# Spread of 1 / rms by float32r identity products, a later gating of the second plain tile, SSM projection chunks of 262, 394 and 392 columns, and another PSUM bank for the last head's norm

## The chip, the core and the metric

The kernel runs on one core of one Trainium2 chip. The metric is the device time of one execution in microseconds (us). The core's engines run side by side, each through its own list of instructions in order: PE (TensorE, matrix products; its weight loads are listed apart as PEld), DVE (VectorE), ACT (ScalarE), POOL (GpSimd) and SP (SyncE, which issues most DMA transfers). An instruction that needs another engine's result waits for it, and everything behind it on its engine waits too.

## The reference, cut to what matters

One step of a hybrid decoder layer on 16 meta tokens, 1024 prompt tokens and 8 sample tokens, 1048 tokens in all, model width 1024:

```python
h = h + 0.5 * swiglu(rmsnorm(h, n1), w1g, w1u, w1d)
u = rmsnorm(h, nm) @ w_in
q, fz, iv, g, z, xbc, dt_raw = jnp.split(u, SPLITS, axis=-1)
...
o_hg = o_hg * lax.rsqrt(jnp.mean(o_hg * o_hg, axis=-1, keepdims=True) + EPS)
o_hg = o_hg.reshape(bsz, seqlen, HG_WIDTH) * hg_norm.astype(f32) * jax.nn.silu(g.astype(f32))
xbc_act, conv_buf = causal_conv(xbc.astype(f32), s_conv.astype(f32), conv_w.astype(f32), conv_b.astype(f32))
...
yz = yz * lax.rsqrt(jnp.mean(yz * yz, axis=-1, keepdims=True) + EPS)
mix = jnp.concatenate([o_hg, yz], axis=-1).astype(h.dtype) @ w_out
h = h + mix
h = h + 0.5 * swiglu(rmsnorm(h, n2), w2g, w2u, w2d)
```

`swiglu(x, wg, wu, wd)` is `(silu(x @ wg) * (x @ wu)) @ wd` with an inner width of 2816. `xbc` (1024 columns) and `dt_raw` (8 columns) are what this page calls the SSM projection. The outputs are the prompt and sample rows after a final norm and the new states.

## The kernel before

Activations are kept transposed: a tile has 128 features on the partitions and tokens along the columns. The token axis has four **quarters** of `Q` = 262 columns in the first half of the kernel (258 after the meta tokens are dropped). Every large product is done as three float32r products (`mm3`, lines 169, 170 and 171): weights and activations are each split into a high part (a cast to float32r, on ACT) and a low part (the rest, a subtraction on DVE), and high x high, high x low and low x high are added up in PSUM. PE therefore needs, for each operand, one ACT and one DVE operation to be done first.

PSUM has two pools here: `mis` with 4 banks (`K.psm()`), and `acc`, with 4 banks outside the feed-forward blocks (`K.psum()`).

**The first feed-forward block** (`ffn`, with `Input` for its input) is written as a list of numbered steps. A step is 12 products of 262 columns on PE; `before(S, i, ...)` places other work ahead of step i, and on one engine the order of these calls is the order of execution. Steps 0 to 31 are two plain tiles (`Plain`): their products run on the input without its norm, since 1 / rms is one number per token and can be multiplied in afterwards. `Input.rms` (step 24) gets 1 / rms of every token, tokens on the partitions; it then writes ten diagonal matrices (`diag`, L1425, on ACT), and `Input.spread_r(q)` (L1430, steps 28 to 31) multiplies a matrix of ones by a quarter of them on PE, in fp32, so that every partition holds 1 / rms along the tokens. L1431 copies that to SBUF. `Plain.late` then multiplies each tile's two halves by it and forms silu(gate) x up (L704, L709, L713 on DVE, 524 columns each; the sub-steps of tile f start at step 33 + 6 f). From step 32 on, pairs of tiles follow (`pair`, `two_pairs`), whose weights are prepared on DVE and ACT at the same time (L493, L497, L501) and whose sums are read from PSUM by DVE (L598, L605, L607, L609).

**From the first block to the SSM projection.** `after1` gets the norm of the block's output a quarter at a time: squares on ACT (L255), sums on DVE (L256), a product with ones on PE (L263), ln and exp on ACT (L185, L186), a Newton step on DVE (L189 to L191), and then eight tiles of normalised x per quarter (`plain_x`: L327 on DVE, L328 high part on ACT, L330 low part on DVE). Quarters 0 and 1 are done during the last steps, quarters 2 and 3 behind them. `ssm_project` multiplies this x by eight units of 128 weight columns. Each unit goes through the token axis in the three chunks of `CHUNKS`, one PSUM bank for each; for the first three units the chunks are the outer loop (`proj_first`), so that chunk 0 of all three comes before chunk 1. `proj_dt` does the 8 columns of dt in the same chunks, and `ssm_decay` (L1540 and after) the small work on dt.

**The last norms.** `Rms` normalises over partitions: `root` sums with four products of 32 output rows (L209) in one bank and takes mean, ln and exp on ACT (L211, L216, L217, with a table load ahead of ln, L214), `newton` has three DVE operations (L221 to L223), and `part` spreads each quarter with one product (L229). Two of them stand at the end of the mixer: that of the SSM group 1 (`ssm_norm`, spreads copied by ACT, L1806) and that of head 3 of the HGRN2 group (`hgrn_out`, spreads read by DVE, L2083). Around them PE works on the first output projection (`out_proj`).

Inside the feed-forward blocks the written order holds for PE, DVE, ACT and SP; in the mixer's middle it holds for PE alone. Elsewhere, at the SSM projection and at the last norms, a scheduler of the language orders the instructions when the kernel is built, from its own estimates. The order on each engine is fixed before the kernel runs.

## Time and profile before

| what | value |
|---|---|
| median of 3 runs | 1921.43 us (1920.21 to 1922.94) |
| the profiled execution | 1922.67 us |
| its span, first to last instruction | 1920.9 us |
| mean granted clock of PE in it | 0.998 |
| PE records, and their busy time | 16692, 1905.5 us |

A row of the timeline has the start of a group of equal instructions in us from the span's start, its length, engine, line, output and input tiles with shapes, and, in brackets, how long the engine had been idle and what released it. Lengths of products overlap: the pace is the distance between two starts. An fp32 product shows two records, a float32r product one. A row of the waits names who waited for whom, for how long in total, how often, and the longest. A row of the stretches has the length, each engine's busy time and number of instructions, the granted clock of PE as a share of full speed, the DMA share and GB/s.

### The profile page before, as it was taken

The page shows a single profiled execution, that of the slowest core. Times are in us where ns is not written, and L with a number is a line of the kernel's source. Part 1 is how long each engine was busy: PE and PEld are TensorE (multiplying, and loading weights), DVE is VectorE, ACT ScalarE, POOL GpSimd, SP SyncE. Part 2 cuts the span into 40 slices and gives each one's busy share as a digit, 9 for nine tenths or more (in the row PEclk, how much of TensorE's full clock was granted, in tenths as well). Part 3 has the DMA queues.
Part 4 walks back from the last instruction along what each step waited for, and adds up shares of the span by engine and source line. Part 5 has one row for each costly group of instructions (what it writes and reads, how often), then busy time and mean ns, then how long its engine had stood idle before and what let it go on. Part 6 is the DMA issues. An engine that isn't in the chain of part 4 may idle for free.

```text
span 1920.9 us, 41195 instructions
## 1 busy us (share of the span) xinstructions
PE 1905.5 (99%) x16692; PEld 1875.2 (98%) x16692; DVE 1526.5 (79%) x2866; ACT 858.0 (45%) x1635; POOL 30.1 (2%) x88
## 2 busy tenths in 40 slices
PE   9999999999999999999999999999999999999998
PEld 9999999999999999999999999999999999999998
DVE  7888888889788877566585557999888888978974
ACT  6533333334534644466564545743333332453353
POOL 3000000000000000000000000000000000000000
PEclk9999999999999999999999999999999999999999
DMA  7143333335967541221463254133333333596852
GB/s 249 50 128 95 95 107 112 92 98 175 305 215 243 165 152 52 66 89 38 116 186 85 83 173 144 58 114 107 99 93 101 101 112 93 173 269 210 281 175 84
DMA packets 324209, 258.46 MB, mean 135 GB/s; under 512 B 18923, under 2 KB 298731, under 8 KB 324011
## 3 DMA queue, kind: packets, MB, share of 16 engines
q1 hardware_dynamic: 323779, 255.79, 43.1%
q8 instruction: 131, 2.15, 0.5%
q14 instruction: 59, 0.48, 0.1%
q0 software_dynamic: 224, 0.04, 0.0%
q10 hardware_dynamic: 16, 0.00, 0.0%
HBM read 190.79 MB, written 65.05 MB: 133 GB/s over the span
## 4 chain that ended last, share of the span: by engine, by line
PE 94%; DVE 3%; ACT 1%; issue 1%; DMA 0%; SPq 0%; DVEq 0%; ACTq 0%
PE acc L169 24%; PE acc L171 23%; PE acc L170 23%; PE mis L169 5%; PE mis L170 5%; PE mis L171 5%; PE mis L1963 1%; DVE u L382 1%; DVE u L367 1%; PE mis L1665 0%; PE mis L2030 0%; PE mis L1659 0%; DMA s<-in_x_prompt_dram 0%; PE mis L2055 0%; PE mis L1654 0%
## 5 line engine op out<-in xcount | busy, mean ns | idle before, releaser
L169 PE MATMUL acc<-u,ws 128*128 128x258 f32 (+4 forms) x3634 | 1064.0, 293 | 1.1 <-DVE u L1279 0.8
L171 PE MATMUL acc<-u,ws 128*128 128x258 f32 (+4 forms) x3634 | 1055.3, 290 | 0.7 <-DVE ws L501 0.7
L170 PE MATMUL acc<-u,ws 128*128 128x258 f32 (+4 forms) x3634 | 1054.8, 290 | 0.0
L169 PEld LDWEIGHTS acc<-u,ws 128*128 128x128 f32 x3634 | 686.5, 189 | 8.7 <-issue 6.2
L170 PEld LDWEIGHTS acc<-u,ws 128*128 128x128 f32 x3634 | 688.3, 189 | 0.8 <-DVE u L330 0.2
L171 PEld LDWEIGHTS acc<-u,ws 128*128 128x128 f32 x3634 | 686.1, 189 | 1.6 <-DVE ws L501 1.1
L169 PE MATMUL mis<-u,ws 128*128 128x262 f32 (+1 forms) x810 | 230.2, 284 | 0.0
L171 PE MATMUL mis<-u,ws 128*128 128x262 f32 (+1 forms) x810 | 228.7, 282 | 0.0
L170 PE MATMUL mis<-u,ws 128*128 128x262 f32 (+1 forms) x738 | 208.6, 283 | 0.0
L501 DVE TENSOR_TENSOR ws<-r,ws 128x512 fp32r<-128x512 f32 x266 | 181.6, 684 | 4.1 <-ACT ws L497 3.9
L901 ACT ACTIVATE t<-t 128x524 f32<-128x524 f32 (+1 forms) x72 | 46.1, 640 | 300.1 <-DVE t L898 300.1
L497 ACT CAST ws<-r 128x512 fp32r<-128x512 f32 x266 | 156.8, 615 | 42.2 <-PE mis L171 18.1
L169 PEld LDWEIGHTS mis<-u,ws 128*128 128x128 f32 x810 | 152.9, 189 | 0.1
L171 PEld LDWEIGHTS mis<-u,ws 128*128 128x128 f32 x810 | 152.7, 189 | 0.0
L170 PEld LDWEIGHTS mis<-u,ws 128*128 128x128 f32 x738 | 139.9, 190 | 0.1
L493 DVE TENSOR_TENSOR r<-r,r 128x512 f32<-128x512 f32 x150 | 100.8, 684 | 0.3
L1031 DVE TENSOR_TENSOR u<-u,u 128x1048 fp32r<-128x1048 f32 (+3 forms) x84 | 96.1, 1146 | 4.8 <-ACT u L1027 4.3
L1089 ACT CAST ws<-u 128x512 fp32r<-128x512 f32 (+1 forms) x72 | 42.1, 585 | 109.9 <-DVE u L1084 105.2
L164 DVE TENSOR_TENSOR ws<-r,ws 128x512 fp32r<-128x512 f32 x88 | 59.5, 685 | 38.3 <-ACT ws L163 38.0
L1027 ACT CAST u<-u 128x1048 fp32r<-128x1048 f32 (+3 forms) x84 | 82.8, 988 | 1.3 <-DMA u<-hd 1.3
L1118 DVE SCALAR_TENSOR_TENSOR s<-acc,s 128x524 f32<-128x524 f32 (+3 forms) x86 | 53.9, 651 | 35.3 <-PE acc L171 35.0
L898 DVE TENSOR_TENSOR t<-t,u 128x524 f32<-128x524 f32 (+1 forms) x108 | 73.2, 692 | 0.1
(465 smaller groups left out, 2329.1 us busy)
## 6 DMA issues: line engine op xcount, KB each, us to landing
r<-in_w_ffn_down_dram SPq DMA_DIRECT2D x128, 256.0 KB
hd<-s SPq DMA_DIRECT2D x93, 258.0 KB
r<-in_w_ffn_gate_dram SPq DMA_DIRECT2D x88, 256.0 KB
r<-in_w_ffn_up_dram SPq DMA_DIRECT2D x88, 256.0 KB
hd<-s SPq DMA_DIRECT2D x77, 262.0 KB
u<-hd SPq DMA_DIRECT2D x36, 516.0 KB
u<-hd SPq DMA_DIRECT2D x28, 524.0 KB
r<-in_w_in_dram SPq DMA_DIRECT2D x56, 256.0 KB
```

Of the source, the lines that this page charges most:

```text
L164: self.nc.vector.tensor_sub(lo, src, hi.bitcast(F32))
L169: mm(ps, whi, xhi, start=first, stop=False, skip_group_check=more)
L170: mm(ps, whi, xlo, start=False, stop=False, skip_group_check=more)
L171: mm(ps, wlo, xhi, start=False, stop=last, skip_group_check=more)
L493: self.K.nc.vector.tensor_tensor(self.raw[p], self.raw[x], self.raw[y], op)
L497: self.K.nc.scalar.copy(self.w[p][:, : self.n * P], self.raw[p])
L501: self.K.nc.vector.tensor_sub(t[:, 512 : 512 + w], self.raw[p], t[:, :w].bitcast(F32))
L898: nc.vector.tensor_mul(t, t if src is None else src, spread.lanes(n, slice(0, 2)))
L901: nc.scalar.activation(t, t, AF.Silu)
L1027: K.nc.scalar.copy(hi, lo.bitcast(F32))
L1031: K.nc.vector.tensor_sub(lo, lo.bitcast(F32), hi.bitcast(F32))
L1118: nc.vector.scalar_tensor_tensor(t, b, 0.5, t, ALU.mult, ALU.add)
```

## The change

The chunks of the SSM projection (all eight units and dt) become 262, 394 and 392 columns:

```diff
+CHUNKS_X = [(0, 262), (262, 394), (656, 392)]
-def proj(K, wh, wl, evac, chunks=CHUNKS):
+def proj(K, wh, wl, evac, chunks=CHUNKS_X):
 def proj_first(K, units):
-    for c in CHUNKS:
+    for c in CHUNKS_X:
 ...
     def proj_dt(c):
-        c0, w = CHUNKS[c]
+        c0, w = CHUNKS_X[c]
```

`Input.rms` no longer writes diagonal matrices. It splits 1 / rms (128 x 10) into a float32r part and a rest, and `spread_r` multiplies one column of each, broadcast over 128 columns as the stationary operand, by columns of a float32r identity matrix that `constants` makes once: for each quarter three pieces (a quarter touches three of the ten token tiles) of two products, 24 products in all. They stand a step later, at steps 29 to 32:

```diff
+    K.identr = cst.tile([P, P], F32R, name="identr")
+    nc.vector.tensor_copy(K.identr, K.ident)
 ...
         token_rstd(K, *(self.st[:, j] for j in range(3)))
-        self.diag = K.slot("u", T)
-        for i, (t0, n) in enumerate(self.tiles):
-            K.nc.scalar.activation(self.diag[:, t0 : t0 + n], K.ident[:, :n], AF.Identity, scale=self.st[:, 1, i : i + 1])
+        self.parts = K.sml.tile([P, 2, 10], F32R, tag="rp", name="rp", bufs=1)
+        K.nc.vector.tensor_copy(self.parts[:, 0], self.st[:, 1])
+        K.nc.vector.tensor_sub(self.parts[:, 1], self.st[:, 1], self.parts[:, 0].bitcast(F32))
     def spread_r(self, q):
         ps = K.psm()[:, :Q]
-        K.nc.tensor.matmul(ps, K.ones[1], self.diag[:, q * Q : q * Q + Q], start=True, stop=True)
+        for i, (t0, n) in enumerate(self.tiles):
+            c0, c1 = max(t0, q * Q), min(t0 + n, q * Q + Q)
+            for j in range(2):
+                if c0 < c1:
+                    K.nc.tensor.matmul(ps[:, c0 - q * Q : c1 - q * Q], self.parts[:, j, i : i + 1].broadcast_to([P, P]), K.identr[:, c0 - t0 : c1 - t0], start=j == 0, stop=j == 1)
         K.nc.scalar.copy(self.spread.quarter(q), ps)
 ...
-            before(S, 28 + q, (x.spread_r, q))
+            before(S, 29 + q, (x.spread_r, q))
```

The gating of the second plain tile starts two steps later, both tiles' gating is placed behind the other work of the same step, and the hidden tiles' sums move with it:

```diff
-                p.late(S, late_r + 6 * f)
-            hidden.jobs(S, 0, hid, late_r + 2, late_r + 10)
+                later.append(lambda p=p, f=f: p.late(S, late_r + 8 * f))
+            later.append(lambda hid=hid: hidden.jobs(S, 0, hid, late_r + 2, late_r + 12))
 ...
+            for fn in later:
+                fn()
+            later = []
```

The root of head 3's norm takes its bank from `acc` in place of `mis`:

```diff
-    def __init__(self, K, v, scale):
-        self.K, self.v, self.scale = K, v, scale
+    def __init__(self, K, v, scale, bank=None):
+        self.K, self.v, self.scale, self.bank = K, v, scale, bank or K.psm
 ...
-        ps = K.psm()[:, :w]
+        ps = self.bank()[:, :w]
 ...
-    rms = Rms(K, v, 1.0 / P)
+    rms = Rms(K, v, 1.0 / P, K.psum if hd == 3 else None)
```

How this moves instructions is shown at three places. In the changed kernel's rows the same code has other line numbers (L169 to L171 are L170 to L172, L209 is L210, L229 is L230, L263 is L264, L1430 is L1440, L1484 is L1494), and the running numbers of the tiles differ.

First PE at the border of the first two chunks of the SSM projection. `u` are the tiles of normalised x (u_8545 and u_8553 are the first tile's high and low part before, u_8559 and u_8567 in the change), `acc` the banks, one for each unit and chunk. Before:

```order
L170 MATMUL acc_9028<-u_8559,ws_8987 128x350
L263 MATMUL mis_8795<-t_8040,ones_85 128x262
L1484 MATMUL mis_8956<-ident,u_8954 128x24 x8
L171 MATMUL acc_9028<-u_8551,ws_8987 128x350
L169 MATMUL acc_9028<-u_8552,ws_8987 128x350
```

In the change:

```order
L171 MATMUL acc_9068<-u_8574,ws_9013 128x262
L172 MATMUL acc_9068<-u_8566,ws_9013 128x262
L264 MATMUL mis_8809<-t_8054,ones_85 128x262
L1494 MATMUL mis_8970<-ident,u_8968 128x24 x8
L170 MATMUL acc_9094<-u_8559,ws_8984 128x394
L170 MATMUL acc_9120<-u_8559,ws_8996 128x394
L170 MATMUL acc_9146<-u_8559,ws_9008 128x394
L171 MATMUL acc_9094<-u_8567,ws_8984 128x394
```

The product for the norm of quarter 2 (L263) and the eight transposes for the convolution (L1484) stood inside the first chunk, with 22 of its products behind them; now they stand behind the whole first chunk, and the second chunk's first products are next.

Second PE at the spread of the first quarter in the first feed-forward block (`rp` holds the two parts of 1 / rms, `mis` the bank). Before, between steps 27 and 28:

```order
L171 MATMUL mis_871<-u_438,ws_609 128x262
L1430 MATMUL mis_886<-u_814,ones_83 128x262
L169 MATMUL acc_825<-u_526,ws_628 128x262
L170 MATMUL acc_825<-u_544,ws_628 128x262
L171 MATMUL acc_825<-u_526,ws_628 128x262
```

In the change, the spreads of quarters 0 and 1 without the steps around them:

```order
L1440 MATMUL mis_893<-identr,rp 128x128 x4
L1440 MATMUL mis_893<-identr,rp 128x6 x2
L1440 MATMUL mis_917<-identr,rp 128x122 x2
L1440 MATMUL mis_917<-identr,rp 128x128 x2
L1440 MATMUL mis_917<-identr,rp 128x12 x2
```

One fp32 product of 262 columns has become six float32r products, of 6 to 128 columns.

Third PE at the two last norms. `t_14251` is 1 / rms of the SSM group before, `t_14265` in the change; `t_14306` is that of head 3 in the change. Before:

```order
L171 MATMUL acc_14381<-u_13582,ws_14331 128x258
L229 MATMUL mis_14260<-t_14251,ones_83 128x258
L229 MATMUL mis_14263<-t_14251,ones_83 128x258
L229 MATMUL mis_14266<-t_14251,ones_83 128x258
L229 MATMUL mis_14269<-t_14251,ones_83 128x258
L209 MATMUL mis_14287<-u_14280,ones_83 32x258 x4
L169 MATMUL acc_14381<-u_13838,ws_14331 128x258
```

In the change (the second root, `acc_14301`, stands 38 rows further up, right behind the first):

```order
L170 MATMUL acc_14395<-u_13596,ws_14345 128x258
L230 MATMUL mis_14274<-t_14265,ones_83 128x258
L230 MATMUL mis_14277<-t_14265,ones_83 128x258
L230 MATMUL mis_14280<-t_14265,ones_83 128x258
L230 MATMUL mis_14283<-t_14265,ones_83 128x258
L230 MATMUL mis_14315<-t_14306,ones_83 128x258
L230 MATMUL mis_14318<-t_14306,ones_83 128x258
L230 MATMUL mis_14321<-t_14306,ones_83 128x258
L230 MATMUL mis_14324<-t_14306,ones_83 128x258
L171 MATMUL acc_14395<-u_13597,ws_14345 128x258
```

The second root has moved ahead of 37 products of the output projection, and head 3's four spreads from 44 products further down to right behind the other four.

More of the change, by code (lines that the diff above doesn't have):

```diff
@@ L1177, in ffn @@
         S.before(32 if plain else 14, lambda: K.banks(2))
-        hidden = Hidden(K)
+        hidden, later = Hidden(K), []
         if plain:
```

## Prediction

> **What bounds the kernel now.** I read the page's busy times and its chain that ended last, then the list of PE's waits, then the timeline around each wait that the change touches.
>
> ```profile
> PE 1905.5 (99%) x16692; PEld 1875.2 (98%) x16692; DVE 1526.5 (79%) x2866; ACT 858.0 (45%) x1635; POOL 30.1 (2%) x88
> ...
> PE 94%; DVE 3%; ACT 1%; issue 1%; DMA 0%; SPq 0%; DVEq 0%; ACTq 0%
> ```
>
> PE is busy for 99% of the span and holds 94% of the chain. So the time changes only by what PE streams more or less of, and by the waits ahead of PE. Those waits are few:
>
> ```profile
> PE acc L169 <- DVE u L1279: 0.8, 1, 0.8
> PE acc L171 <- DVE ws L501: 0.7, 2, 0.4
> ...
> PE mis L209 <- ACT s L1806: 0.4, 1, 0.4
> ```
>
> The change aims at each of them, and at two at L1430 that are quoted below. So each part has the same question: when this wait goes, which one is next?
>
> **Part 1, the SSM projection's chunks.** First the pace of a product: two rows that are 23 products of 262 columns apart, two that are 11 of 350 columns apart, and the entry of the projection.
>
> ```profile
> 682.31 0.28 PE L169 MATMUL acc<-u,ws 128*128 128x262 f32 x1
> ...
> 685.10 0.28 PE L171 MATMUL acc<-u,ws 128*128 128x262 f32 x1
> ...
> 698.67 0.28 PE L171 MATMUL acc<-u,u 128*128 128x262 f32 x1
> 699.74 0.59 PE L169 MATMUL acc<-u,ws 128*128 128x350 f32 x2 [0.78 <-DVE u L1279]
> ...
> 722.68 0.33 PE L169 MATMUL acc<-u,ws 128*128 128x350 f32 x1
> ...
> 724.46 0.32 PE L171 MATMUL acc<-u,ws 128*128 128x350 f32 x1
> ```
>
> A product of 262 columns takes 2.79 / 23 = 0.121 us, one of 350 takes 1.78 / 11 = 0.162 us: in proportion to the columns, as far as these rows tell. All three chunks together have the same columns and the same number of products as before, so streaming gains and loses nothing. What changes is when each operand is needed. The old first chunk (columns 0 to 349) needs quarters 0 and 1 of the normalised x, and PE waits for quarter 1 from 698.79 (698.67 plus one product) to 699.74, and 0.2 more in the next products: 1.2 us. The new first chunk is quarter 0 alone, which is ready, so PE goes on at once. But both the old second chunk (350 to 699) and the new one (262 to 655) reach into quarter 2 (524 to 785). When quarter 2 is ready is told by its chain:
>
> ```profile
> 706.46 0.42 DVE L1118 SCALAR_TENSOR_TENSOR s<-acc,s 128x262 f32<-128x262 f32 x1
> ...
> 706.98 0.42 ACT L255 ACTIVATE t<-s 128x262 f32<-128x262 f32 x1 [0.93 <-DVE lb L1287]
> ...
> 707.42 1.28 ACT L179 ACT_TABLE_LOAD   x1
> 707.43 0.43 DVE L256 TENSOR_TENSOR t<-t,t 128x262 f32<-128x262 f32 x1 [0.27 <-ACT t L255]
> ...
> 708.07 0.60 PE L263 MATMUL mis<-t,ones 128*128 128x262 f32 x2
> 708.61 0.67 PE L1484 MATMUL mis<-ident,u 24*128 24x24 f32 x8
> ...
> 709.48 0.53 ACT L186 ACTIVATE t<-t,lna 128x262 f32<-128x262 f32 x1
> ...
> 711.83 0.90 DVE L327 SCALAR_TENSOR_TENSOR t<-s,col,t 128x262 f32<-128x262 f32 x2
> 712.36 0.82 ACT L328 CAST u<-t 128x262 fp32r<-128x262 f32 x2 [1.75 <-DVE t L327]
> ```
>
> The chain starts on DVE behind quarter 1's tiles and runs DVE, ACT, PE, ACT, DVE, ACT. PE's only link in it, L263 at 708.07, comes right after DVE's L256 ends at 707.86, and the ACT step behind it waits for the table load to 708.70 anyway. DVE's order is the same in the change up to here, so starting PE earlier doesn't start this chain earlier: the first high part of quarter 2 lands at about 712.8 in both kernels. Before, PE reached the second chunk at that very moment, busy throughout. Now: 72 products of 0.121 from 698.8 end at 707.5; the norm's product and the eight transposes (held to 708.07 by L256) end at 709.2; then PE has nothing in its order until 712.8. That is a wait of about 3.6 us, and 0.5 ahead of L263. At 712.8 the old kernel had 72 products of 0.162 behind it, the new one 72 of 0.121: **+2.9 us**, and the 1.2 us at the entry are already in it (they only make the new wait longer). PE's order is fixed, and ahead of quarter 2's first product it holds nothing more. Later DVE delivers one tile of eight in about 0.75 us and the interleaved order uses about 4 products of 394 columns (0.18 each, by proportion) for it, so PE isn't starved again.
>
> The clock is the second half of this part.
>
> ```profile
> 743.82 1.28 PE L1540 MATMUL mis<-sel,u 16*128 16x8 f32 x10
> ...
> 744.00:747.40 3.40, 3.40 (x28) 3.11 (x28) 1.89 (x6) 2.46 (x3) 0.00 (x0) 1.00 0.52 139
> 747.40:750.80 3.40, 3.40 (x12) 3.40 (x13) 3.30 (x13) 0.27 (x1) 0.00 (x0) 0.50 0.60 162
> 750.80:754.20 3.40, 3.40 (x22) 3.40 (x22) 2.92 (x15) 0.45 (x1) 0.00 (x0) 1.00 0.29 85
> ```
>
> After 3.4 us in which most records are 8-column scraps, the granted clock is 0.50 for 3.4 us, and 12 products run where the next stretch has 22: (22 - 12) x 0.162 = 1.6 us lost. In the change PE would stream only some 0.6 us between 707.5 and 712.8, thinner than that stretch, so I expect the clock to halve once: between 0.8 us (half of the stretch falls into the wait) and 2.5 us (a second stretch), I take **+1.6**. If instead only a stretch without any work halves the clock, the wait of 3.6 us would hardly ever cover a whole one of 3.4, and the term is 0; the stretch ahead of 747.4 wasn't without work, so I follow the row and keep the other as a rival. The Trainium skill ("TensorE: Matmul & The Clock Gate", Part 1 and "HAM oscillation — how this bites in real kernels") speaks for that rival: it has the gate look at free-running windows of about 3.4 us and warns of idle gaps above that length, by which the sum would lose its 1.6.
>
> **Part 2, the spread of 1 / rms.** The four fp32 products and what surrounds them:
>
> ```profile
> 59.77 0.28 PE L171 MATMUL mis<-u,ws 128*128 128x262 f32 x1
> 60.45 0.71 PE L1430 MATMUL mis<-u,ones 128*128 128x262 f32 x2 [0.40 <-ACT u L1425]
> ...
> 64.24 0.28 PE L171 MATMUL acc<-u,ws 128*128 128x262 f32 x1
> 65.02 0.71 PE L1430 MATMUL mis<-u,ones 128*128 128x262 f32 x2 [0.49 <-ACT u L1431]
> ...
> 67.59 0.28 PE L170 MATMUL mis<-u,ws 128*128 128x262 f32 x1
> ```
>
> From 59.77 to 67.59 are 7.82 us with 38 main products, which take 38 x 0.121 = 4.6; so 3.2 us go to the spread. The waits are 60.45 - 59.89 = 0.56 and 65.02 - 64.36 = 0.66; the products are the other 2.0. Both waits go: the ten ACT pieces are gone, one step more lies ahead, and DVE gets two operations of 10 columns in their place, a step before they are read. The new price is 24 products with a 128-column stationary operand, 16 of 122 to 128 columns and 8 of 6 or 12. No float32r product under 256 columns is in the trace. Low: 128 columns in proportion to 262, 0.06 each, 24 x 0.06 = 1.4. Nearest row: the ten L1540 records above also have 128 stationary columns and stream only 8; they take 1.28 us with the last one's tail, so about 0.12 each, and 24 x 0.12 = 2.9. High: the fp32 price, two such records for each wide product, 16 x 0.24 + 8 x 0.12 = 4.8. I take 2.9, as the stationary operand has the same width: 2.9 - 3.2 = **-0.3**, from -1.8 to +1.6.
>
> **Part 3, the gating two steps on.** It moves three of DVE's 524-column operations behind the weight's low half that PE waited for.
>
> ```profile
> 78.00:107.70 29.70, 29.26 (x239) 28.93 (x237) 29.53 (x49) 10.67 (x19) 0.00 (x0) 1.00 0.33 105
> ...
> 87.26 0.39 PE L171 MATMUL acc<-u,ws 128*128 128x262 f32 x1 [0.44 <-DVE ws L501]
> ...
> 107.05 0.69 DVE L607 TENSOR_TENSOR t<-acc,t 128x524 f32<-128x524 f32 x1
> ...
> 107.89 0.36 PE L169 MATMUL acc<-u,ws 128*128 128x262 f32 x1
> ```
>
> The wait ahead of 87.26 (0.6 us) goes. But DVE is busy 29.53 of 29.70 us here, and from the start of this stretch to the read of the bank at 107.05 the change has the very same operations, in another order. PE's product at 107.89 waits for that read, so PE arrives earlier and waits longer: **0**. If DVE weren't the limit there, the gain would be the 0.6 plus the two waits behind it, 0.9.
>
> **Part 4, the last norm's bank.**
>
> ```profile
> 1147.72 1.28 ACT L214 ACT_TABLE_LOAD   x1
> 1149.01 0.42 ACT L216 ACTIVATE t<-t 128x258 f32<-128x258 f32 x1
> 1149.46 0.51 ACT L217 ACTIVATE t<-t,lna 128x258 f32<-128x258 f32 x1
> ...
> 1151.29 0.43 DVE L223 SCALAR_TENSOR_TENSOR t<-t,t 128x258 f32<-128x258 f32 x1
> ...
> 1151.87 0.72 PE L229 MATMUL mis<-t,ones 1*128 1x258 f32 x8
> 1153.00 0.64 PE L209 MATMUL mis<-u,ones 128*32 128x258 f32 x8 [0.42 <-ACT s L1806]
> ```
>
> The second root (L209) no longer waits for a bank, so the 0.46 us between the two rows go. But PE's order now has all eight spreads in a row, and the last four need the second norm's Newton steps. On ACT these come after the first norm's exp, which ends at 1149.97 in the row and some 0.2 later behind the second root's copy, and after another table load of 1.28: with ln (0.42) and exp (0.51) they end at 1152.4. Three DVE operations of 0.46 (L223 and the two ahead of it) give 1153.8. PE is through with the first four spreads at 1152.59 in the row, and 0.3 later now (the root of 0.57 ahead of them, two products fewer): a new wait of 0.9. So 0.9 - 0.46 = **+0.4**, from -0.5 (no new wait) to +0.8.
>
> **Sum.** +2.9 + 1.6 - 0.3 + 0 + 0.4 = +4.6 us. Against the profiled execution (1922.67, span 1920.9 and 1.8 around it) that is 1927.3. That execution holds the half-clock stretch at 747.4, which need not fall into every run; the median of the runs shown is 1921.43, so I forecast **1926.0**.
>
> **Rivals.**
> - *The wait comes, the clock stays* (only a stretch without any work halves it): +2.9 - 0.3 + 0.4 = +3.0, 1924.4. For it: the gap is broken by the norm's product at 708.07. Against: the row at 747.4.
> - *Narrow float32r products cost the fp32 price*: 4.8 - 3.2 = +1.6 in place of -0.3, 1927.9. For it: nothing in the trace but fp32 at this width; against: each fp32 product shows two records, a float32r one shows one.
> - *Not slower: quarter 2 isn't late.* If its chain is released by PE and moves up with it, the entry's 1.2 us are kept and no wait and no half clock follow: -1.2 - 0.3 + 0.4 = -1.1, 1920.3. It decides once quarter 2's first cast ends before 709.2. Against: DVE's L1118 at 706.46 sits behind quarter 1's tiles.
> - *The gating's gain stays* (DVE reaches L607 earlier): -0.9, 1925.1.
>
> **How the numbers follow.** Forecast 0.55, clock stays 0.20, narrow price 0.13, not late 0.07, gating 0.05. Measurements of this kernel tell 0.2% (3.8 us) from no change, so slower means above 1925.27: the forecast's upper 70% (0.39), nearly all of the narrow price (0.12) and a little of the rest (0.04) make 0.55; within 0.2% is 0.42; faster needs two rivals at once, 0.03. The range: down to 1922.5 (clock stays, with spread at its low bound), up to 1928.6 (second stretch of half clock, or the narrow price).
>
> **What would show it.** Right: a wait of 3 to 4 us on PE after the eight 24-column transposes, ended by the cast of quarter 2; a stretch at 0.50 clock behind it; no wait at the projection's entry, nor at the spread; a longer wait near 107; about 1 us of wait among the eight spreads near 1153. Wrong: quarter 2's cast earlier by more than 1 us, or PE filling the gap with other products.

## The result, and the profile after

| | before | changed |
|---|---|---|
| median (us) | 1921.82, 6 executions, 1920.21 to 1923.08 | 1930.51, 6 executions, 1927.76 to 1932.03 |
| span of the profiled execution (us) | 1920.9 | 1929.1 |

The ratio is 1.0045, with a 95% interval of 1.0032 to 1.0058: 8.7 us slower, between 6.1 and 11.1. The forecast was 1926.0, 4.6 us slower than the kernel before. The direction is right, and the time lies above the range.

The page of the changed kernel (its busy times, and its chain of work that ended last) reads as before: PE sets the end.

```profile
PE 1908.8 (99%) x16708; PEld 1879.8 (97%) x16708; DVE 1526.7 (79%) x2869; ACT 855.8 (44%) x1625; POOL 32.5 (2%) x88
...
PE 93%; DVE 4%; ACT 2%; DMA 1%; issue 1%; DVEq 0%; SPq 0%; ACTq 0%
```

PE's waits in the changed kernel (who waited for whom, total, times, longest):

```profile
PE acc L170 <- ACT u L329: 3.5, 1, 3.5
PE mis L1640 <- DVE s L1665: 2.1, 2, 2.0
...
PE mis L230 <- DVE t L224: 1.4, 1, 1.4
...
PE acc L170 <- DVE t L608: 0.5, 1, 0.5
```

The first is the border of the chunks, the third the eight spreads of the last norms, the fourth the gating: all three forecast. The second stands in the SSM scan, which the change does not touch. (`ssm_scan` goes through nine blocks of 128 tokens. For each, SP loads `cumd`, a small table of cumulated decays, spread over the partitions: one transfer at L1622, two at L1629. ACT reads the first at L1647.)

To see where the time goes, take the start of the same PE product in both profiles:

| place | before | changed | later by | since the row above |
|---|---|---|---|---|
| a transpose of the input (L1343) | 15.36 | 14.59 | -0.76 | -0.8 |
| first main product after the four spreads | 70.75 | 69.56 | -1.19 | -0.4 |
| product after the late read of the bank | 107.89 | 106.80 | -1.09 | +0.1 |
| a norm's product (L263) | 644.18 | 644.27 | +0.09 | +1.2 |
| norm of quarter 2 (L263) | 708.07 | 708.12 | +0.05 | 0.0 |
| dt's first small product (L1540) | 743.82 | 748.11 | +4.29 | +4.2 |
| a transpose ahead of the scan (L1526) | 808.01 | 810.84 | +2.82 | -1.5 |
| in the SSM scan (L1654) | 849.05 | 855.65 | +6.60 | +3.8 |
| in the last HGRN2 scan (L1975) | 1107.86 | 1115.03 | +7.17 | +0.6 |
| a norm's product in the second block (L263) | 1197.49 | 1204.83 | +7.33 | +0.2 |
| a transpose near the end (L2135) | 1847.97 | 1856.18 | +8.21 | +0.9 |

The border costs 4.2, the scan 3.8. The -1.5 behind the border is the old half-clock stretch at 747, which this execution does not have; seven of the sixteen profiles here (before, changed, e1 to e14) have one between 745 and 753. The 1.2 from 108 to 644 and the 0.9 at the end build up where PE's order is the same in both kernels and nothing waits.

The border, in the changed kernel's timeline of PE and in three stretches around it:

```profile
708.12 0.71 PE L264 MATMUL mis<-t,ones 128*128 128x262 f32 x2 [0.26 <-DVE t L257]
708.76 0.67 PE L1494 MATMUL mis<-ident,u 24*128 24x24 f32 x8
712.98 1.03 PE L170 MATMUL acc<-u,ws 128*128 128x394 f32 x2 [3.55 <-ACT u L329]
```

```profile
709.42:712.83 3.41, 0.01 (x1) 0.00 (x0) 3.15 (x9) 0.98 (x3) 0.00 (x0) 1.00 0.00 0
713.20:716.60 3.40, 3.40 (x12) 3.40 (x13) 3.40 (x10) 1.78 (x5) 0.00 (x0) 0.55 0.00 0
716.60:720.00 3.40, 3.40 (x21) 3.40 (x20) 3.19 (x9) 1.24 (x3) 0.21 (x4) 1.00 0.02 5
```

PE stands still until 712.98, where the forecast had 712.8, and runs 12 products where the next stretch has 21. The half clock begins at 712.83; the 3.41 us ahead of it hold 0.01 us of PE work.

The scan, in the changed kernel's timeline of SP, ACT and PE:

```profile
836.34 0.33 SPq L1622 DMA_DIRECT2D s<-cumd  x1
837.34 1.23 SPq L1629 DMA_DIRECT2D s<-cumd  x2
```

```profile
842.69 2.44 ACT L1647 ACTIVATE s<-s,s 128x128 f32<-128x128 f32 x8 [3.12 <-DMA s<-cumd]
```

```profile
846.02 0.60 PE L1632 MATMUL mis<-ident,u 128*128 128x128 f32 x4
848.58 0.44 PE L1640 MATMUL mis<-ident,u 128*128 128x128 f32 x2 [1.96 <-DVE s L1665]
```

and the same load and its reader in the kernel before:

```profile
833.50 0.33 SPq L1612 DMA_DIRECT2D s<-cumd  x1
```

```profile
837.33 2.46 ACT L1637 ACTIVATE s<-s,s 128x128 f32<-128x128 f32 x8 [0.60 <-DMA s<-cumd]
```

ACT gets the load 6.35 us after its issue, before 3.8. ACT's exp and DVE's L1665 follow it, L1665 frees the bank that PE's next transposes need, and PE stops for 2.0. The transfers between 837 and 846 of the changed kernel (GB/s in 40 slices, and the queue that fetches instructions), then GB/s of the kernel before at the same distance from its issue (834.16 to 843.16):

```profile
GB/s 0 146 364 309 382 55 0 0 73 164 330 314 332 296 237 121 118 118 66 16 18 18 20 23 20 20 7 0 0 0 0 0 0 0 0 0 0 0 0 0
...
q8 instruction: 1, 0.02, 0.7%
```

```profile
GB/s 0 146 146 364 346 455 309 184 205 205 264 212 175 225 173 121 7 0 0 5 9 9 9 0 0 0 0 0 0 0 36 0 0 0 0 0 0 0 0 0
```

In the changed kernel the load stops for about half a microsecond near 838.5 and ends in a thin tail of 16 to 23 GB/s up to 843; before, it runs through. A packet of the instruction queue, 16 KB and 0.97 us long, starts at 838.93, behind the stop and ahead of the tail. Whether it makes the load late isn't told by these rows; e7 tests it.

### The profile page after: what moved, and what is told of

The parts are those of the page before. It is cut to its first block, busy times and chain, and to the rows that moved or that the text cites. A ratio compares the mean times of both kernels' runs of the same rounds, so it can differ in the third digit from the quotient of the medians.

```text
span 1929.1 us, 41213 instructions
## 1 busy us (share of the span) xinstructions
PE 1908.8 (99%) x16708; PEld 1879.8 (97%) x16708; DVE 1526.7 (79%) x2869; ACT 855.8 (44%) x1625; POOL 32.5 (2%) x88
## 4 chain that ended last, share of the span: by engine, by line
PE 93%; DVE 4%; ACT 2%; DMA 1%; issue 1%; DVEq 0%; SPq 0%; ACTq 0%
PE acc L170 24%; PE acc L172 23%; PE acc L171 23%; PE mis L170 5%; PE mis L172 5%; PE mis L171 5%; PE mis L1973 1%; DMA s<-cumd 1%; PE mis L2040 0%; DVE ws L502 0%; PE mis L2065 0%; PE mis L1962 0%; PE mis L1669 0%; DVE t L328 0%; PE mis L2067 0%
## 5 line engine op out<-in xcount | busy, mean ns | idle before, releaser
L170 PE MATMUL acc<-u,ws 128*128 128x258 f32 (+6 forms) x3634 | 1065.8, 293 | 4.4 <-ACT u L329 3.5
L172 PE MATMUL acc<-u,ws 128*128 128x258 f32 (+6 forms) x3634 | 1056.8, 291 | 0.5 <-DVE ws L502 0.3
L171 PE MATMUL acc<-u,ws 128*128 128x258 f32 (+6 forms) x3634 | 1054.8, 290 | 0.0
L170 PEld LDWEIGHTS acc<-u,ws 128*128 128x128 f32 x3634 | 687.3, 189 | 11.6 <-issue 6.4
L171 PEld LDWEIGHTS acc<-u,ws 128*128 128x128 f32 x3634 | 688.3, 189 | 0.6 <-issue 0.3
L172 PEld LDWEIGHTS acc<-u,ws 128*128 128x128 f32 x3634 | 686.2, 189 | 1.1 <-DVE ws L502 0.9
L172 PE MATMUL mis<-u,ws 128*128 128x262 f32 (+1 forms) x810 | 229.8, 284 | 0.0
L170 PE MATMUL mis<-u,ws 128*128 128x262 f32 (+1 forms) x810 | 229.6, 283 | 0.0
L171 PE MATMUL mis<-u,ws 128*128 128x262 f32 (+1 forms) x738 | 208.5, 283 | 0.0
L170 PEld LDWEIGHTS mis<-u,ws 128*128 128x128 f32 x810 | 153.3, 189 | 0.0
L172 PEld LDWEIGHTS mis<-u,ws 128*128 128x128 f32 x810 | 152.7, 188 | 0.0
L171 PEld LDWEIGHTS mis<-u,ws 128*128 128x128 f32 x738 | 139.8, 189 | 0.0
```

Source lines behind the costliest of these rows:

```text
L170: mm(ps, whi, xhi, start=first, stop=False, skip_group_check=more)
L171: mm(ps, whi, xlo, start=False, stop=False, skip_group_check=more)
L172: mm(ps, wlo, xhi, start=False, stop=last, skip_group_check=more)
```

## The experiments

Times are medians. The kernel before ran beside each group, with 1921.3 to 1922.2 us.

| run | us | ratio to before | 95% interval |
|---|---|---|---|
| e1 changed kernel again | 1932.01 | 1.0053 | 1.0040 to 1.0065 |
| e2 chunks alone | 1928.17 | 1.0031 | 1.0020 to 1.0043 |
| e3 changed, old chunks | 1928.82 | 1.0036 | 1.0022 to 1.0050 |
| e4 changed, four chunks | 1927.57 | 1.0030 | 1.0019 to 1.0042 |
| e5 changed, rp of 128 bytes | 1928.29 | 1.0038 | 1.0026 to 1.0051 |
| e6 a tile of 80 bytes alone | 1923.02 | 1.0009 | 1.0000 to 1.0018 |
| e7 16 more PE records alone | 1925.26 | 1.0020 | 1.0011 to 1.0029 |
| e8 changed, old spread | 1927.65 | 1.0034 | 1.0021 to 1.0047 |
| e9 four chunks and spread | 1923.38 | 1.0010 | 1.0001 to 1.0019 |
| e10 bank alone | 1923.28 | 1.0008 | 0.9999 to 1.0017 |
| e11 gating alone | 1922.20 | 1.0002 | 0.9993 to 1.0012 |
| e12 spread alone, rp of 128 bytes | 1924.17 | 1.0014 | 1.0005 to 1.0023 |
| e13 two units in four chunks | 1923.33 | 1.0006 | 0.9997 to 1.0015 |
| e14 the same and the spread | 1922.34 | 1.0000 | 0.9991 to 1.0009 |

### The changed kernel again (e1), no edit

> The changed kernel as it is, looked at a second time. The first profile of it shows two new stops of PE: 3.46 us at 709.2 (the border of the first two chunks, with a half-clock stretch of 3.4 us behind it) and 2.13 us at 846.4 (in the SSM scan, behind a load of cumd that took some 6.3 us from its issue where the others take 3.7 to 4.1; with a second half-clock stretch behind it). Theory 'border': only the first belongs to the change and the late load is chance: this profile has the wait at 709 and none over 0.5 us near 846, and a span of about 1925. Rival 'scan': the late load comes with the change: the wait of about 2 us near 846 is there again, and the span is about 1929. Timed: 8 to 9 us over the kernel before in both, if the medians of six runs hold.

The scan's wait is there, but of 0.2 us, and the span is 1928.1 nevertheless: a half-clock stretch that lasted 3.4 us behind the border in the first profile lasts 6.8 here, and another stands at 753. The load near 839 takes 4.6 us from issue to landing, where the first profile's took 6.3. So the late load is neither pure chance nor always as late. Both theories miss a part.

### The chunks alone (e2), and all but the chunks (e3)

```diff
 e2: the kernel before, with
+CHUNKS_X = [(0, 262), (262, 394), (656, 392)]
 (as in the change)
 e3: the changed kernel, with
-CHUNKS_X = [(0, 262), (262, 394), (656, 392)]
+CHUNKS_X = CHUNKS
```

> The kernel before with the chunks of 262, 394 and 392 alone. Theory 'border': the wait of some 3.5 us, 0.4 ahead of the norm's product and the half clock behind it cost 4.5 against the old entry; with a half-clock stretch of the old kernel at 747 gone in some runs: 3 to 5 us over the kernel before. Rival 'scan': another 3.7 from the wait near 846: 7 to 9 us. Rival 'elsewhere': if most of the 8.7 us comes from the other three parts, under 3 us.

> The changed kernel with the old chunks of 350, 350 and 348 (spread, gating and bank stay changed). In the first two profiles, set side by side, the spread gained 0.4, the gating gave 0.1 back beyond its gain, the bank cost 0.1 to 0.2: theory 'border' and rival 'scan' both give -0.5 to +0.5 us against the kernel before. Rival 'elsewhere': 4 us or more over it, with a wait that the first profile of the changed kernel doesn't show as new.

The chunks cost 6.2 us, a little above the 3 to 5 of "border". The profile says why in part: two stretches of half clock behind the wait. (It is of the fastest of the six executions, 1926.54; what the median has beyond that no profile shows.)

```profile
708.50:711.90 3.40, 0.59 (x8) 0.49 (x8) 2.56 (x8) 1.22 (x4) 0.00 (x0) 1.00 0.14 56
711.90:718.70 6.80, 6.07 (x18) 6.07 (x19) 6.59 (x18) 3.47 (x9) 0.12 (x4) 0.50 0.00 0
718.70:722.10 3.40, 3.40 (x20) 3.40 (x20) 1.01 (x3) 0.71 (x3) 0.10 (x3) 1.00 0.06 3
```

PE worked for 0.59 us of the stretch ahead of the half clock. It is 0.6 to 0.7 in e1 and e8, which have two stretches as well, and nothing in e5, which has one like the changed kernel. So in these five profiles two follow where the wait covers only a part of the 3.4 us ahead, and one where it covers them whole.

E3 is the surprise: without the chunks the kernel is still 6.8 us slower, which "border" and "scan" both put near 0. Its profile has none of the border's waits, but two in the scan (0.81 and 1.22, at 845 and 864) and a half-clock stretch at 898. (E10 and e11 have one at 892 without these waits, so it need not come from them.) So the scan's waits don't come with the chunks.

### Pace and addresses (e5, e6)

The new tile `rp` (80 bytes a partition, laid out as 96) and the identity (512) move the tiles behind them in SBUF: the activations `u`, PE's moving operands, start 608 bytes later, the weights `ws`, which lie ahead of `rp`, 512. In e5 `u` starts 640 bytes later and `ws` the same 512; in e6 `u` starts 96 bytes later and `ws` stays.

```diff
 e5: the changed kernel, with
-self.parts = K.sml.tile([P, 2, 10], F32R, tag="rp", name="rp", bufs=1)
+self.parts = K.sml.tile([P, 2, 16], F32R, tag="rp", name="rp", bufs=1)[:, :, :10]
 e6: the kernel before, with (in Input.rms)
+pad = K.sml.tile([P, 2, 10], F32, tag="rp", name="rp", bufs=1)
+K.nc.gpsimd.memset(pad, 0.0)
```

> The changed kernel, its new tile rp laid out with 128 bytes a partition in place of 80, so that the activations' tiles behind it start 640 bytes later than in the kernel before (a multiple of 64) in place of 608 (not one). Nothing else differs. In the feed-forward blocks, where the order of PE is the same in all kernels, the pace of a product was 0.12166 us (120 to 400 us of the span) and 0.12169 (400 to 640) before and with the chunks alone, and 0.12198 and 0.12190 in the three profiles that have the new spread. Theory 'address': the pace is set by where the moving operand starts; it is 0.12166 and 0.12169 here again, and the time is about 2 us below the changed kernel (1929 to 1930 where that has 1930.5 to 1932). Rival 'spread itself': the pace comes from the new operations or the identity's 512 bytes; 0.12198 and 0.12190 again, and no gain.

> The kernel before with a tile of 80 bytes a partition at the place where rp would be, set to zero by POOL and never read: the activations' tiles start 96 bytes later, and no other instruction changes. Theory 'address': pace 0.1219 to 0.1220 in the first feed-forward block, and 2 us over the kernel before. Rival 'spread itself': pace 0.12166 and 0.12169, and the time of the kernel before.

Three stretches, in which PE is never idle, in the kernel before, the changed kernel, e5 and e6; the first (x...) is the number of PE's products:

```profile
120.00:400.00 280.00, 280.00 (x2304) 280.00 (x2303) 242.29 (x440) 90.22 (x168) 0.00 (x0) 1.00 0.33 100
400.00:640.00 240.00, 240.00 (x1974) 240.00 (x1974) 204.89 (x323) 105.29 (x175) 0.00 (x0) 1.00 0.68 211
1300.00:1850.00 550.00, 550.00 (x4587) 550.00 (x4586) 472.21 (x802) 203.03 (x355) 0.20 (x1) 1.00 0.49 150
```

```profile
120.00:400.00 280.00, 280.00 (x2298) 280.00 (x2297) 241.50 (x439) 90.25 (x168) 0.00 (x0) 1.00 0.33 99
400.00:640.00 240.00, 240.00 (x1972) 240.00 (x1971) 204.39 (x323) 105.52 (x175) 0.00 (x0) 1.00 0.68 211
1300.00:1850.00 550.00, 550.00 (x4581) 550.00 (x4580) 476.41 (x809) 202.56 (x352) 0.20 (x1) 1.00 0.50 152
```

```profile
120.00:400.00 280.00, 280.00 (x2307) 280.00 (x2306) 242.62 (x441) 90.22 (x168) 0.00 (x0) 1.00 0.33 99
400.00:640.00 240.00, 240.00 (x1974) 240.00 (x1973) 204.74 (x323) 106.60 (x177) 0.00 (x0) 1.00 0.69 213
1300.00:1850.00 550.00, 550.00 (x4586) 550.00 (x4585) 474.35 (x805) 202.22 (x352) 0.20 (x1) 1.00 0.49 151
```

```profile
120.00:400.00 280.00, 280.00 (x2304) 280.00 (x2303) 242.29 (x440) 90.22 (x168) 0.00 (x0) 1.00 0.33 100
400.00:640.00 240.00, 240.00 (x1970) 240.00 (x1969) 204.40 (x323) 105.40 (x175) 0.00 (x0) 1.00 0.68 210
1300.00:1850.00 550.00, 550.00 (x4582) 549.94 (x4581) 472.04 (x802) 202.75 (x354) 0.20 (x1) 1.00 0.49 150
```

The changed kernel does 6, 2 and 6 products fewer in the same time (0.7, 0.2 and 0.7 us). E1 and e3 have its counts to within one, and e2 the counts before up to 640. In the third stretch e2, with the old starts, has 4581 too: the stretch begins there at another place in PE's order, so its counts alone prove nothing. Between the same two products of PE's order (those at 120 and 640 and at 1300 and 1850 in the kernel before) the differences are clean:

| longer than before (us) | 120 to 640 | 1300 to 1850 |
|---|---|---|
| e2 | 0.0 | 0.1 |
| changed, e1, e3 | 1.15 | 0.7 |
| e5 | -0.3 | 0.1 |
| e6 | 0.5 | 0.6 |

E5 differs from the changed kernel only in where the tiles behind `rp` start, and has the old pace or a better one: "address" holds, for 1.8 us in the changed kernel. In time e5 is 7.0 us over the kernel before where the changed kernel was 8.7 and 10.0, which agrees, but the intervals overlap. E6 is 1.7 us slower, with an interval that begins at zero. Its first 280 us keep the old pace, though its tiles start at the same places modulo 64 bytes as the changed kernel's, so the theory as written is half right there: the start modulo 64 is not all that counts.

Sorted by where the moving operand starts, the 262-column products from 120 to 640 take (ns from one start to the next, 990 to 1114 products each; the start addresses are those of each kernel's layout):

| start, modulo 64 bytes | 0 | 8 | 16 | 24 | 32 | 40 | 48 | 56 |
|---|---|---|---|---|---|---|---|---|
| before | | | 121.1 | | 121.6 | 122.4 | | 121.7 |
| e5 | | | 121.0 | | 121.8 | 122.3 | | 121.5 |
| changed | 122.3 | 122.3 | | 122.6 | | | 120.7 | |
| e6 | 122.2 | 121.9 | | 122.5 | | | 120.6 | |

Each start belongs to one of the four 262-column pieces of a tile (32 and 0 to the first, 56 and 24 to the second, 16 and 48 to the third, 40 and 8 to the fourth). So the table compares two starts for each piece: 0 and 24 are slower than 32 and 56, the other two pairs differ by 0.5 or less.

### PE's instruction fetches (e7, e12, and the rows of all)

PE's program is fetched in pieces of about 256 instructions: the traces have 131 packets of 16 KB in the instruction queue for some 33,400 rows of products and weight loads. A product and its weight load are two. The spread adds 16 records of each ahead of the scan, 32 instructions, so every later fetch comes 16 products earlier in the program.

```diff
 e7: the kernel before, with (in spread_r, into the unused part of the bank)
+for _ in range(2):
+    K.nc.tensor.matmul(bank[:, 400:408], K.ones[1], self.diag[:, 0:8], start=True, stop=True)
 e12: the kernel before, with the change's spread, rp as in e5
```

> The kernel before with two more fp32 products of 8 columns behind each of the four spreads (16 more records on PE, as many as the change's spread adds); nobody reads what they write. By the transfers of the profiles PE's own program is fetched 256 instructions at a time, about 1 us each on one of the engines that also carry the cumd loads; before, such a fetch fell 3.4 to 4.2 us behind the issue of every second cumd load in the SSM scan, with the change's 32 further instructions (a product and a weight load each) 0 to 2.6 us behind it. Theory 'fetch': the 32 instructions alone do that; fetches 0 to 2.6 us behind the issues of cumd between 825 and 880, PE waits of 0.4 to 2.4 us in all at the third to fifth chunk of the scan (near 846 and 865), in some runs a half clock behind them; with the products' own 1.3 to 2.0 us that is 2.5 to 6 us over the kernel before. Rival 'chance': late loads fall anywhere; no wait of over 0.2 us in the scan, and 1.3 to 2.0 us over the kernel before.

> The kernel before with the new spread alone, rp laid out with 128 bytes so that the pace stays. Theory 'fetch': the spread itself gains 0.4, PE's fetches fall 0 to 3 us behind the issues of cumd, and PE waits 0.4 to 2.4 us in the scan, in some runs with a half clock behind it: +0.5 to +3.5 us over the kernel before, with fetches at 0 to 3 us in the profile. Rival 'no price beside the pace': -0.4 us, no wait in the scan.

Three or four fetches fall near the loads of `cumd` that are issued between 823 and 877. How long each starts behind the issue of a load, and what PE then waits in the scan:

| kernel | instructions added ahead of the scan | fetch behind issue (us) | PE's wait (us) |
|---|---|---|---|
| before | 0 | 4.2, 3.5, 3.4 | 0 |
| e2, e6, e8, e10, e11 | 0 | 2.5 to 4.2 | 0 |
| changed | 32 | 2.6, 0.7, 0.4 | 2.1 |
| e1 | 32 | 0.9, 3.5, -0.1 | 0.2 |
| e3 | 32 | 0.9, 0.1, -0.1 | 2.0 |
| e5 | 32 | 0.9, 2.9, 0.0 | 1.1 |
| e7 | 32 | 0.7, 0.1, -0.7 | 0.4 |
| e12 | 32 | 0.9, 0.6, 0.0 | 0.4 |
| e13 | 96 | 6.2, 4.8, 4.3, 3.3 | 0 |
| e14 | 128 | 5.6, 3.6, 3.3, 0.9 | 0 |
| e4, e9 | 208 | 0.2, 6.9, 6.3, 4.3 | 0 |

E7 is the clean dose: nothing but 16 records that nobody reads moves the fetches as forecast, and the wait comes.

```profile
843.65 0.44 PE L1633 MATMUL mis<-ident,u 128*128 128x128 f32 x2 [0.42 <-DVE s L1658]
```

All six profiles with 32 instructions show a wait of PE in the scan, none of the ten others does. (In e4 the fetch at 0.2 falls on the load issued at 825; there ACT waits 0.97 for it, and PE doesn't. In e14 the fetch at 0.9 falls on a load issued at 876.5, which lands 3.1 us after its issue; PE doesn't wait.)

The loads themselves say the same. In the sixteen profiles 98 loads (those of the first transfer of a block) are issued between 820 and 876. The 80 that no fetch follows within 2.6 us (or precedes by up to 0.1; bounds taken from the table) land 2.7 to 4.1 us after their issue; the 18 that one does take 3.5 to 6.3, and 13 of them longer than any of the 80. So a fetch close behind the issue goes with a late load, though not every time. How the one delays the other isn't shown.

The spread alone, with the pace kept, costs 2.8 us (interval 1.0 to 4.4), e7 4.0 (2.1 to 5.6), of which its own products are 1.0. But e7's profile is of the fastest of its eleven executions (1922.64) and e12's of one of the faster (1922.53), each with a wait of 0.4: that longer waits and half clock make up the rest in the median is argued, not shown. How late the load gets differs from one execution to the next, from 0.2 to 2.1 us of wait in the same program.

### Old spread (e8), bank alone (e10), gating alone (e11)

```diff
 e8: the changed kernel, with the diagonals, the four fp32 products and their step of before
 e10: the kernel before, with
+    rms = Rms(K, v, 1.0 / P, K.psum if hd == 3 else None)
 e11: the kernel before, with
+                later.append(lambda p=p, f=f: p.late(S, late_r + 8 * f))
```

> The changed kernel with the old spread (ten diagonals, four fp32 products, a step earlier); chunks, gating and bank stay changed. Theories 'address' and 'fetch' together: pace 0.12166 and 0.12169, no wait over 0.2 us in the scan, the border's waits of 3.46 and 0.4 with one or two half-clock stretches as with the chunks alone, the wait of 1.7 among the eight spreads near 1154: 0 to 1.5 us over the chunks alone, so 1928 to 1930. Rival 'neither': the time of the changed kernel, 1930.5 to 1932.

> The kernel before with the last head's root in a bank of acc alone. In seven profiles with this edit the wait among the eight spreads is 1.7 us, the piece of PE's order around it takes 0.1 to 0.2 us longer, and three of the seven have a half-clock stretch right behind it (1.6 us). Theory 'wait and half clock': +0.2 in executions without the stretch, +1.8 with it: median +0.3 to +1.5 us over the kernel before. Rival 'the wait alone': within 0.3 us of it.

> The kernel before with the later gating of the second plain tile alone. The prediction's theory (DVE sets the end of this stretch): the wait of 0.6 at 87 goes, one of 0.5 comes near 107, and the time is within 0.5 us of the kernel before. Rival (the gain stays): 0.6 to 0.9 us below it.

E8 is as expected up to its time: old pace, no wait in the SSM scan, and 1927.65, just below its 1928 to 1930. Bank and gating, added to the chunks, so add nothing that these runs can tell. Its spreads show what the bank can do (PE's timeline, then three stretches):

```profile
1158.18 0.79 PE L230 MATMUL mis<-t,ones 1*128 1x258 f32 x8 [1.35 <-ACT s L1810]
```

```profile
1155.30:1158.70 3.40, 2.05 (x24) 1.33 (x22) 2.96 (x7) 2.51 (x7) 0.00 (x0) 1.00 0.39 140
1158.70:1162.10 3.40, 3.40 (x19) 3.20 (x16) 3.40 (x7) 1.05 (x2) 0.00 (x0) 0.50 0.16 36
1162.10:1165.50 3.40, 3.40 (x30) 3.40 (x30) 2.25 (x6) 2.10 (x3) 0.00 (x0) 1.00 0.32 125
```

A wait of 1.35 is followed by a stretch at half clock; 19 products in place of 30 (the shorter ones of 258 columns) are 1.3 us. E4 and e5 have it too; the changed kernel, e1, e3 and e10 have the same wait without it. Alone the bank costs 1.9 us, and its interval (-0.2 to 3.3) leaves open whether that is anything. The gating costs 0.8 (-1.3 to 2.3): nothing that these runs can tell, as forecast.

### Without the border (e4, e9, e13, e14)

```diff
 e4: the changed kernel, with
+CHUNKS_X = [(q * Q, Q) for q in range(4)]      (first three units and dt; the others use CHUNKS)
 e9: the kernel before, with these chunks and the spread of e12
 e13: the kernel before, with the first two units in four quarters, the third in 262, 394, 392
 e14: e13 with the spread of e12
```

> The changed kernel with four chunks of 262 for the first three units and for dt, and the old 350, 350, 348 for the other five units. The second chunk is then quarter 1 alone: 72 products of 0.121 from 707.5 to 716.2, by when quarter 2's first cast (712.8) is done. Theory 'border': no wait over 0.5 us and no half clock near 709, so 4.1 to 4.5 less than the changed kernel, and the entry's 1.2 us of the kernel before saved too: -1.5 to 0 us against the kernel before. Rival: the wait moves to the border of the second and third chunk (quarter 3, or a bank that is not yet read): over 1 us there, and less than half of the gain.

> The kernel before with the new spread (rp laid out with 128 bytes, so that the activations' tiles start a multiple of 64 bytes later) and with four chunks of 262 for the first three units and dt; old gating, old bank, old chunks in the other five units. Theory, all parts together: spread -0.4, entry of the projection -1.2, pace as before, PE's fetches 6 to 8 us behind the cumd loads as in the earlier run with four chunks, so no wait in the scan; no new half clock: -2.5 to -0.5 us against the kernel before. Rival: what the run with four chunks lost (5.6 over the kernel before) lay in none of these: 2 us or more over it.

> The kernel before with the first two units of the SSM projection in four chunks of 262 and the third in 262, 394, 392; dt and the other five units in the old chunks, nothing else changed. PE's order then holds 48 products of 262 on quarter 1 (707.5 to 713.3) between the first chunk and quarter 2's first cast at 712.8. It adds 96 instructions to PE ahead of the SSM scan, by which the fetches fall some 5 us behind the issues of the cumd loads. Theories 'border' and 'fetch': no wait over 0.3 us at the entry, at the border and in the scan, and no new half clock: -1.5 to -0.5 us against the kernel before. Rival: a fetch falls on another place where PE uses its instructions up fast (with four chunks in three units PE stopped 2.4 us at 1109 with nothing to wait for but itself), and the time is that of the kernel before or above.

> The same chunks with the new spread, its tile rp laid out with 128 bytes: 128 instructions more on PE ahead of the scan, so the fetches fall some 3 us behind the issues of cumd, on the load before, as in the kernel before. Theories: spread -0.4, entry -1.2, no wait over 0.3 us in the scan: -2 to -0.5 us against the kernel before. Rival: as for the other kernel, the time of the kernel before or above.

With quarter 1 as a chunk of its own the wait of 3.5 is gone in all four, which settles its cause: PE had nothing else to do until quarter 2's cast. But none is faster than the kernel before: e4 is 5.6 us over it, e9 2.0, e13 1.2 and e14 0.2, where 0 to 2.5 below it was expected. In e4's profile the new pace is 2.5 of it, and the bank's place with a half clock 2.2. E9 and e13 stop elsewhere, as e13's rival had it, and the profile shows nothing that PE waits for ("issue"):

```profile
1043.32 0.43 PE L169 MATMUL acc<-u,ws 128*128 128x344 f32 x1
1045.10 0.31 PE L170 MATMUL acc<-u,ws 128*128 128x344 f32 x1 [1.35 <-issue]
```

Ahead of these rows PE runs 66 products of 8 or 16 columns, 132 instructions, in about 0.6 us, while a fetch started at 1042.53. In e9 the like happens at 1109 for 2.3 us, with a fetch at 1109.34. That PE lacks instructions there fits, but is argued. E14 has neither stop and takes the time of the kernel before, not the 0.5 to 2 us less that were expected: in its profile and e13's the entry gains 0.5 by dt's first small product, not 1.2.

## Why the prediction was right or wrong

- **The border's wait** ("about 3.6 us, and 0.5 ahead of L263"): right, 3.55 in the row and 0.26 ahead of L264 (0.42 beyond the pace of the starts), ended by the cast of quarter 2.
- **The clock** ("halve once", 1.6, with 2.5 for a second stretch): right in mechanism and in size. Behind the border the changed kernel and e5 have one stretch, e1, e2 and e8 two. From 708.07 to 743.82 of the kernel before, one makes it 4.2 us later (the changed kernel, e5), where 2.9 + 1.6 is 4.5; two make it 5.3 to 5.5, where 2.9 + 2.5 is 5.4. The rival that the clock stays is out, but not by the first profile: there the wait does cover a whole stretch (0.01 us of work), which the prediction thought would hardly ever happen, so the rival too has a half clock there. E1, e2 and e8 decide it, with 0.6 to 0.7 us of work ahead of the half clock. The Trainium skill ("TensorE: Matmul & The Clock Gate", Part 1) lets the gate close after an idle window of about 3.4 us. The changed kernel and e5 fit that; e1, e2 and e8 don't, nor do the changed kernel's scan (1.5 us of work in the 3.4 ahead) and the stretch at 1155 (2.05).
- **The spread** (-0.3): right at its place, -0.4. The six products from 60.68 take 0.1 each, as the rows below show; the fp32 price is out.

```profile
60.68 0.73 PE L1440 MATMUL mis<-identr,rp 128*128 128x128 f32 x6
61.26 0.37 PE L170 MATMUL acc<-u,ws 128*128 128x262 f32 x1
```

- **The gating** (0): right. The wait near 87 goes, and 0.50 come at 106.80, ended by the same read of the bank.
- **The bank** (+0.4): the wait is 1.35 where 0.9 was forecast, since the first four spreads end earlier than I had them; the place as a whole costs 0.2. The half clock that sometimes follows was not in the sum.
- **The step that failed is the sum**: "+2.9 + 1.6 - 0.3 + 0 + 0.4". It prices each edit by the instructions that it puts in or moves, and leaves out what the spread changes for all the others: its tiles shift the operands' addresses (1.8 us in the two parts measured, gone in e5), and its 32 instructions shift PE's fetches onto the loads of the scan (2.1 and the half clock behind it in the first profile, 0.2 in the second). Neither has a term in the sum. No row of the profile before showed either, and no part of the prediction asked for them. In the two profiles the terms of the sum come to 4.2 - 0.4 + 0.1 + 0.2 = 4.1, near the forecast 4.6; the rest is the scan (3.8, and 0.6 behind it) and the pace (1.2 and 0.9), less the 1.5 at 747 and 0.8 at the start: 8.2 in all, but for rounding. The base made no difference: 1927.3, from the profiled execution, is too low as well. The range's ends don't follow from its reasons either: the spread's low bound gives 1922.9, the second stretch 1926.9 and the narrow price 1927.9, where it has 1922.5 and 1928.6.
- **The rivals**: quarter 2 is late, so "not late" is out; "the gating's gain stays" too.

What stays open: the parts don't seem to add. Chunks, spread, pad, bank and gating alone cost 6.2, 2.8, 1.7, 1.9 and 0.8, 13.4 together, and the change 8.7 to 10.0. Each of these has an interval of some 2 us either way, so the gap may be noise; the stretches of half clock, which come and go with where a wait falls, may account for it too; no run separates that. Nor is it known what about an operand's start sets the pace, or how a fetch makes a load late: in the one load shown the stop begins 0.6 us ahead of the fetch's packet.

## What to carry to other kernels

An edit on a saturated engine can have two prices that its own rows don't show: the bytes that it adds to SBUF, which can move the operands of later products, and the instructions that it adds, which move the fetches of the program against the transfers. So compare first the time between the same two products where the order is unchanged: if it differs, look at the layout before the edit. And a wait of some microseconds on PE is to be priced with one or two stretches of half clock behind it, even if a few products interrupt it.

## What the runs showed of the hardware that was not expected

- The pace of a product can depend on where its moving operand starts: with `u` 608 bytes further on, the changed kernel takes 1.15 us longer in 520 us and 0.7 in 550; with 640 (e5) it is -0.3 and 0.1. By start and piece of the tile the means run from 120.6 to 122.6 ns for 262 columns.
- PE's program comes in 16 KB pieces, about 1 us each, among the packets of the core's 16 DMA engines. The Trainium skill ("Runtime: NRT & Kernel Launch", Instruction fetch mechanics) gives blocks of 256 instructions, which the traces bear out, and calls their cost mostly hidden; here it does not seem so, with waits of up to 2.1 us behind loads that a fetch meets, and stops of 1.35 and 2.3 us of PE that look like a want of instructions.
- A stretch of 3.4 us in which PE works for 2.05 can be followed by half clock, and another execution with the same wait goes without.
